# Pairing neighbouring attention-logit steps in two pairs of PSUM banks

## The chip, the cores and the metric

The kernel runs on one core of one Trainium2 chip. A core has five engines with a queue each: TensorE (PE, matmuls, with its weight loads shown as PEld), VectorE (DVE), ScalarE (ACT), GpSimd (POOL) and SyncE (SP), which issues the DMA transfers. The engines run on their own and meet through semaphores. Matmul results land in PSUM, which the kernel uses as eight banks of 128 x 512 fp32. The metric is the time of one execution on the device, in microseconds (us), as the median of the runs.

## What is computed

Two encoder layers run over a sequence of 512 tokens of width 1024. Layer 0 mixes tokens by differential attention, layer 1 by gated linear attention; in both, a four-head cross-attention into 256 memory tokens runs beside the mixer, then one output projection and a gated MLP follow. The change is in layer 0. Its mixer, cut to what matters:

```python
def diff_attention(q, k, v, ...):          # 6 heads, each with two maps m of width 64
    q = rms_norm(q, g0) * d ** -0.5; k = rms_norm(k, g1)
    for each block of 128 queries:
        logits = einsum('bhmqd,bhmkd->bhmqk', qb, k) + bias
        logits = where(key_chunk <= query_chunk, logits, -inf)
        p = softmax(logits)
        w = p[:, :, 0] - lam * p[:, :, 1]
        o = einsum('bhqk,bhkv->bhqv', w, v)
    return rms_norm(o, g) * (1 - lam_init)
```

The memory cross-attention has heads of width 64 as well, with logits of 128 queries by 256 memory tokens.

## The kernel before

All large products (the projections, the output projection, the MLP) split their fp32 operands into a high and a low part and issue three matmuls of 128x128 weights by 512 columns for each. These are called gemm matmuls here (lines L330 to L332 in `gemm`, L351 to L353 in `product`). The weights come from DRAM in blocks of 128x1024 or less; ScalarE makes the high part (L253) and VectorE the low part (L256).

In layer 0 the attention is woven into the gemm matmuls of the projections by a script, `SCRIPT`, read by `do` from left to right. A number fills in that many microseconds' worth of gemm matmuls from a queue `F` (by its own costing). A letter with a number issues one step. TensorE executes in exactly this order. The other engines' queues are ordered by the framework's scheduler when the program is built. The steps:

- `P` (`prepare`): four transposes of a head's q and four of its k on TensorE (helper at L220), each into one `ps_tp` bank; ScalarE copies each bank out (L682).
- `L` (`logits`, step t of 15): 64-row matmuls (L719), since a map has width 64. The two maps go to the upper and lower 64 rows and to two banks, tag `lg`. The steps group (head, query block) pairs so that one step fills up to 512 columns (`TOGETHER`); each step is 8, 12 or 16 matmul instructions on the chip. VectorE then adds the bias and finds the maximum, bank by bank (L726), ScalarE takes the exponential (L729), VectorE combines the two maps (L734, L735, L738).
- `T` (`turn`): four transposes of the combined weights into a `ps_tp` bank, copied out by ScalarE (L748).
- `V` (`values`): eight matmuls with v (L760) into an `sm` bank. The last `V` of a head starts `output`: four squares on ScalarE (L771).
- `s` (scale): VectorE normalises the head's output (L777, L779).
- `F` (`finish`): four transposes of a finished head into a `ps_tp` bank. ScalarE (L310) and then VectorE (L311) read it to make the high and low part for the output projection.
- `q`, `k`, `l`, `t`, `v`: the same for the memory cross-attention: normalisation (q0: L386, L387, L390) and transposed queries (q1, two groups of four transposes into `ps_tp`, copied at L582), keys into an `sm` bank, logits (L591, 64-row matmuls, eight per block, maximum at L599, exponential at L603), transposes into `ps_tp` (L616), values (L629).
- `N`, `a`, `b`, `X`, `O`, `!`: normalisation of q and k, operands of the memory projection, reloading x, the output projection (its sums are added at L1061), flushing the queue.

PSUM has four tags, `mm`, `sm`, `lg` and `tp`, with two banks each. A bank is free for the next user of its tag once its readers are done. `M`, `logits` with the tag `tp`, is defined among the steps and not used by the script.

In layer 1 the memory logits are issued two blocks at a time, one block in the `lg` banks and one in the `sm` banks.

Of the kernel before, what the change touches and what calls it, by code (L numbers as in the profile page):

```python
# [37 lines left out]

SCRIPT = """
    17.75 P0 3.9  # L40
    L0 a3 P1 8.45 a0 0.97
    L1 1.94 a1 T0
    L2 3.57 a2
    L3 T1 4.86 N2 V0 T2 N3 V1 12.33
    L4 P2 6.17 V2 T3
    L5 s0 T4 2.27 V3
    L6 P3 b1 V4 5.2 T5
    L7 T6 F0 7.14 b0
    L8 V5 T7 8.42 V6 s1 N5 N4 F1
    L9 V7 P4 b2 4.45 T8 T9 s2 3.0  # L50
    L10 V8 3.55 X P5 q0
    L11 b3 V9 T10 4.2
    L12 F2 V10 s3 T11 3.8 q1 k0
    L13 3.15 l0 V11 T12 3.65
    L14 F3 t0 3.3 V12 T13 t1 l1 3.9 T14 l2 t2 2.3 O k1 t3 s4 l3 v0 t4 V13 V14 t6 t5 1.3 t7 F4 v1 s5 F5 6.15 ! 4.55
"""

ORDER = (('v', 0), ('qk', 1), ('kv', 0), ('qk', 2), ('vm', 2), ('kv', 1))
# [28 lines left out]
def _pieces():  # L87

    plan = []

    def piece(key, name, i, ks, *ranges):
        plan.append((key, name, i, ks, ranges))

    for l in range(2):
        if l == 0:
            w = "w_in_diff"
            piece(("qk", 0), w, 0, K8, (0, 256), (768, 1024))
            for key in ORDER:
                if key[0] == "qk":
                    p = key[1]  # L100
                    piece(key, w, 0, K8, (256 * p, 256 * p + 256), (768 + 256 * p, 1024 + 256 * p))
                elif key[0] == "kv":
                    piece(key, "w_mem_kv", key[1], K8, (0, 512))
                elif key[0] == "vm":
                    p = key[1]
                    piece(key, w, 0, K8, (1536 + 256 * p, 1792 + 256 * p), (2304, 2560))
                else:
                    p = key[1]
                    piece(key, w, 0, K8, (1536 + 256 * p, 2048 + 256 * p))
        else:  # L110
            w = "w_in_gla"
            piece(("gm", 1), w, 0, K8, (2304, 2576))
            for c in range(5):
                piece(("g", c), w, 0, K8, (512 * c, min(512 * c + 512, 2304)))
        for i, part in enumerate(PASS[l]):
            for c, ks in part:
                piece(("o", l, i, c), "w_out", l, ks, (256 * c, 256 * c + 256))
        base = 0
        for nq in HALVES:
            for q in range(base, base + nq):  # L120
                piece(("ua", l, q), "w_up", l, K8, (256 * q, 256 * q + 256))
                piece(("ug", l, q), "w_up", l, K8, (DFF + 256 * q, DFF + 256 * q + 256))
            for c in range(4):
                piece(("dn", l, base, c), "w_down", l, tuple(range(2 * base, 2 * base + 2 * nq)),
                      (256 * c, 256 * c + 256))
            base += nq
    return plan


def _blocks():  # L130

    out = []
    for key, name, i, ks, ranges in _pieces():
        w = sum(b - a for a, b in ranges)
        step = WTILE // w
        out.append([(name, i, ks[j:j + step], ranges, w) for j in range(0, len(ks), step)])
    return out
# [42 lines left out]
def trunk(ctx, tc, head_d, x_t, mem_t, wpack, cols_a_d, cols_d, conv_d, gate_d, rel_bias, diff_lambda, consts, onehot, out):  # L180
# [12 lines left out]
    def bank(tag):  # L193
        return ps.tile([128, 512], F32, name=f"ps_{tag}", tag=tag)

    def xtile():
        return xs.tile([128, S], F32, name="xt", tag="xs", bufs=XS)
# [9 lines left out]
    def blk(b, w=128):  # L207
        return slice(w * b, w * b + w)
# [40 lines left out]
    plan, blocks, made = _pieces(), _blocks(), []  # L249
# [318 lines left out]
    class MemAttn:  # L568
# [13 lines left out]
                A.activation(self.qT[hp], p, AF.Copy, scale=c_mq(self.l))  # L582


        def logits(self, *blocks):
            banks = [(bank(tag), bank(tag)) for _, tag in zip(blocks, ("lg", "sm") if self.l else ("lg", "tp"))]
            for b, pl in zip(blocks, banks):
                for hp in range(2):
                    for j in range(2):
                        hh = blk(j, 64)  # L590
                        mm(pl[j][:, blk(hp, 256)], self.qT[hp][hh, blk(b)], kmT[self.l][hh, hp], start=True, stop=True)  # L591
            for b, pl in zip(blocks, banks):
                self.softmax(b, pl)
# [51 lines left out]
    def diff_layer(pool, mix, acc):  # L645
# [45 lines left out]
        def members(t):  # L691
            pr, s = divmod(t, len(TOGETHER))
            out, at = [], 0
            for j, i in TOGETHER[s]:
                out.append((2 * pr + j, i, 4 * j + i, at))
                at += 128 * (i + 1)
            return pr, out, at

        def bias(h):
            bt = heads[h]["bt"] = pool.tile([128, S], F32, name="bt", bufs=2)  # L700
            src = bass.AP(tensor=bias_d.tensor, offset=bias_d[h].offset + 1, ap=[[1, 128], [1, 512]])
            nc.sync.dma_start(bt, src)
            G.memset(bt[0:64, 0:64], -1e30)

        def logits(t, tag="lg"):
            pr, group, _ = members(t)
            P = pairs[pr]
            s2, nm, rc = P["s2"], P["nm"], P["rc"]
            for h, _, _, _ in group:
                if "bt" not in heads[h]:  # L710
                    bias(h)
            pls = bank(tag), bank(tag)
            for h, i, _, at in group:
                nk = 128 * (i + 1)
                cuts = (0, nk) if i == 0 else (0, nk // 2, nk)
                for k0, k1 in zip(cuts, cuts[1:]):
                    for m in range(2):
                        hh = blk(m, 64)
                        mm(pls[m][:, at + k0:at + k1], heads[h]["q"][hh, blk(i)], heads[h]["k"][hh, k0:k1],  # L719
                           start=True, stop=True)  # L720
            e = xtile(), xtile()
            for m in range(2):
                for h, i, g, at in group:
                    c = slice(at, at + 128 * (i + 1))
                    n1 = nm[:, 8 * m + g:8 * m + g + 1]
                    V.tensor_tensor_reduce(  # L726
                        out=e[m][:, c], in0=pls[m][:, c], in1=heads[h]["bt"][:, 127 + 128 * i::-1], scale=-1.0,
                        scalar=1e38, op0=ALU.add, op1=ALU.min, accum_out=n1)
                    A.activation(e[m][:, c], e[m][:, c], AF.Exp, scale=-1.0, bias=n1,  # L729
                                              accum_out=s2[:, m, g:g + 1])  # L730
            ids = sorted(g for _, _, g, _ in group)
            step = max(ids[-1] - ids[0], 1)
            b, lr = slice(ids[0], ids[-1] + 1, step), slice(8 + ids[0], 9 + ids[-1], step)
            V.reciprocal(rc[:, b], s2[:, 1, b])  # L734
            V.scalar_tensor_tensor(rc[:, lr], rc[:, b], nlam, s2[:, 0, b], op0=ALU.mult, op1=ALU.mult)  # L735
            for _, i, g, at in group:
                c = slice(at, at + 128 * (i + 1))
                V.scalar_tensor_tensor(e[1][:, c], e[1][:, c], rc[:, 8 + g:9 + g], e[0][:, c],  # L738
                                                    op0=ALU.mult, op1=ALU.add)
            live[t] = e[1]  # L740
# [57 lines left out]
        ma = MemAttn(pool, 0, qm, mix, False)  # L798
        ops, keys = [None] * 2, [None] * 2
        for key in ORDER:  # L800
# [16 lines left out]

        doing = {
            "L": logits, "M": lambda i: logits(i, "tp"), "T": turn, "V": values, "P": prepare, "F": finish,
            "N": lambda i: norms(i // 2, i % 2), "a": lambda i: ops[0]((2 * i, 2 * i + 1)),  # L820
            "b": lambda i: ops[1]((2 * i, 2 * i + 1)), "k": lambda i: keys[i]("sm"),
            "q": lambda i: ma.queries() if i else (F.need("v2"), ma.norm()),
            "l": lambda i: ma.logits(i), "t": ma.turn, "v": lambda i: ma.values(i, "sm"),
            "s": lambda i: scales.pop(i)(), "X": lambda i: load_x(x_t),
            "O": lambda i: last.append(out_proj(0, mix, 1, acc, 5)), "!": lambda i: F.flush()}
        do(SCRIPT, doing)
# [228 lines left out]
    def load_x(src):  # L1055
        for k in range(KT):
            xT[k] = xtile()
            nc.sync.dma_start(xT[k], src[k])
# [117 lines left out]
    for l in range(2):  # L1176
        with tc.tile_pool(name=f"at{l}", bufs=2) as pool:
            mix = [None] * 8
            sums, acc = acc, [None]
            if l == 0:  # L1180
                diff_layer(pool, mix, acc)
            else:
                gla_layer(pool, mix, sums)
                out_proj(1, mix, len(PASS[1]) - 1, acc)
                F.flush()
        with tc.tile_pool(name=f"ff{l}", bufs=2) as pool:
            acc = ffn(pool, l, acc)
# [73 lines left out]
```

## Time and profile before

| | |
|---|---|
| median of 3 runs | 1168.48 us (1168.42 to 1168.51) |
| the profiled execution | 1168.01 us |
| its span, first to last instruction | 1166.2 us |
| mean granted TensorE clock | 1.000 |
| logit matmuls of layer 0 (L719) | 168, first at 53.3, last at 188.3 us |

The profile of one execution gives the span in several views: busy time of each engine, the chain of work that ended last, groups of instructions by line, operation and tile ("out<-in", then the shapes, the count, the busy time and the mean duration in ns, and the idle time before them), and the order in time (start, duration, engine, line, operation, tiles, shapes, count; neighbouring equal instructions are merged). Matmuls overlap: the end of one is modelled, so the spacing of starts tells how long TensorE spends on each.

### The profile page before, as it was taken

How to read it: one execution, taken by the hardware profiler on the slowest of the kernel's cores; microseconds unless marked ns; L12 is line 12 of the kernel's file. 1: busy time of each engine (PE TensorE's matmuls, PEld its weight loads, DVE VectorE, ACT ScalarE, POOL GpSimd, SP SyncE). 2: the span in 40 equal slices, each digit the busy share in tenths (PEclk: the TensorE clock that was granted, in tenths of full speed). 3: DMA queues.
4: the chain of work that ended last, by engine and by line, in shares of the span. 5: the costliest groups of instructions: out<-in, count | busy, mean ns of one | idle time of the engine just before them, and what ended most of it. 6: DMA issues, size and time to landing. Idle time of an engine off the chain costs nothing.

```text
span 1166.2 us, 14790 instructions
## 1 busy us (share of the span) xinstructions
PE 1160.7 (100%) x5658; PEld 965.3 (83%) x5658; DVE 750.9 (64%) x1256; ACT 545.5 (47%) x951; POOL 5.0 (0%) x27
## 2 busy tenths in 40 slices
PE   9999999999999999999999999999999999999998
PEld 7888888888888888888888888988888888888887
DVE  7576778688677326677447637777876743576741
ACT  6676687555344213344437634436643421343420
POOL 0000000000000000000000000000000000000000
PEclk9999999999999999999999999999999999999999
DMA  8423242123223223222342230333232323232231
GB/s 295 158 70 99 78 141 73 63 103 130 85 90 120 83 88 124 75 91 98 120 148 68 81 108 3 110 121 109 93 123 73 98 102 108 85 114 73 89 101 45
DMA packets 39556, 117.68 MB, mean 101 GB/s; under 512 B 4703, under 2 KB 7192, under 8 KB 39486
## 3 DMA queue, kind: packets, MB, share of 16 engines
q1 hardware_dynamic: 39054, 116.35, 29.5%
q8 instruction: 44, 0.72, 0.3%
q10 hardware_dynamic: 432, 0.39, 0.1%
q14 instruction: 26, 0.21, 0.1%
HBM read 112.52 MB, written 4.21 MB: 100 GB/s over the span
## 4 chain that ended last, share of the span: by engine, by line
PE 98%; ACT 1%; DVE 1%; issue 0%; POOL 0%; DVEq 0%; POOLq 0%
PE ps_mm L352 9%; PE ps_mm L351 9%; PE ps_mm L353 9%; PE ps_sm L353 8%; PE ps_sm L352 8%; PE ps_sm L351 7%; PE ps_mm L330 6%; PE ps_mm L332 6%; PE ps_mm L331 6%; PE ps_tp L353 3%; PE ps_lg L353 3%; PE ps_lg L352 3%; PE ps_tp L352 3%; PE ps_lg L351 3%; PE ps_tp L351 3%; PE ps_tp L220 3%
## 5 line engine op out<-in xcount | busy, mean ns | idle before, releaser
L253 ACT CAST whi<-raw 128x1024 fp32r<-128x1024 f32 (+4 forms) x212 | 207.6, 986 | 245.4 <-PE ps_tp L352 120.9
L256 DVE TENSOR_TENSOR wlo<-raw,whi 128x1024 fp32r<-128x1024 f32 (+4 forms) x212 | 240.3, 1140 | 117.5 <-ACT whi L253 116.6
L351 PE MATMUL ps_mm<-xsh,whi 128*128 128x512 f32 x438 | 171.6, 392 | 0.0
L352 PE MATMUL ps_mm<-xsl,whi 128*128 128x512 f32 x438 | 170.6, 389 | 0.0
L353 PE MATMUL ps_mm<-xsh,wlo 128*128 128x512 f32 x438 | 170.5, 389 | 0.0
L351 PE MATMUL ps_sm<-xsh,whi 128*128 128x512 f32 x378 | 147.0, 389 | 0.0
L352 PE MATMUL ps_sm<-xsl,whi 128*128 128x512 f32 x378 | 147.0, 389 | 0.0
L353 PE MATMUL ps_sm<-xsh,wlo 128*128 128x512 f32 x378 | 147.0, 389 | 0.0
L330 PE MATMUL ps_mm<-whi,xsh 128*128 128x512 f32 (+2 forms) x336 | 129.1, 384 | 0.0
L332 PE MATMUL ps_mm<-whi,xsl 128*128 128x512 f32 (+2 forms) x336 | 126.1, 375 | 0.0
L331 PE MATMUL ps_mm<-wlo,xsh 128*128 128x512 f32 (+2 forms) x336 | 125.9, 375 | 0.0
L1113 ACT ACTIVATE cvo<-u,cv 128x512 f32<-128x512 f32 x88 | 71.4, 815 | 112.1 <-DVE u L1111 112.1
L352 PEld LDWEIGHTS ps_mm<-xsl,whi 128*128 128x128 f32 x438 | 82.3, 188 | 17.2 <-DVE xsl L311 0.4
L351 PEld LDWEIGHTS ps_mm<-xsh,whi 128*128 128x128 f32 x438 | 82.2, 188 | 17.1 <-issue 0.3
L353 PEld LDWEIGHTS ps_mm<-xsh,wlo 128*128 128x128 f32 x438 | 82.2, 188 | 17.1
L1114 DVE SCALAR_TENSOR_TENSOR cvo<-u,cv,cvo 128x512 f32<-128x512 f32 x88 | 65.7, 749 | 36.2 <-ACT cvo L1113 36.0
L352 PEld LDWEIGHTS ps_sm<-xsl,whi 128*128 128x128 f32 x378 | 70.9, 188 | 14.8
L351 PEld LDWEIGHTS ps_sm<-xsh,whi 128*128 128x128 f32 x378 | 70.9, 188 | 14.7
L353 PEld LDWEIGHTS ps_sm<-xsh,wlo 128*128 128x128 f32 x378 | 70.9, 188 | 14.7
L332 PEld LDWEIGHTS ps_mm<-whi,xsl 128*128 128x128 f32 x336 | 63.2, 188 | 11.6
L330 PEld LDWEIGHTS ps_mm<-whi,xsh 128*128 128x128 f32 x336 | 63.2, 188 | 11.3 <-ACT ks L659 0.3
L331 PEld LDWEIGHTS ps_mm<-wlo,xsh 128*128 128x128 f32 x336 | 63.3, 188 | 10.4
(295 smaller groups left out, 1760.1 us busy)
## 6 DMA issues: line engine op xcount, KB each, us to landing
raw<-in_wpack_dram SPq DMA_DIRECT2D x178, 512.0 KB, 3.5
xt<-in_x_t_dram SPq DMA_DIRECT2D x15, 256.0 KB, 5.2
raw<-in_wpack_dram SPq DMA_DIRECT2D x15, 256.0 KB, 3.0
raw<-in_wpack_dram SPq DMA_DIRECT2D x8, 384.0 KB, 3.0
xres<-xt SPq DMA_DIRECT2D x8, 256.0 KB, 3.0
xt<-xres SPq DMA_DIRECT2D x8, 256.0 KB, 5.4
out_dram<-xt SPq DMA_DIRECT2D x7, 256.0 KB, 2.0
bt<-bias_d SPq DMA_DIRECT2D x6, 256.0 KB, 4.1
```

The lines of the kernel that those rows point to most:

```text
L220: nc.tensor.transpose(dst, src, ident[:n, :n])
L253: ins = A.copy(hi[:, c], raw[:, c])
L256: V.tensor_sub(lo[:, c], raw[:, c], hi[:, c].bitcast(F32))
L330: mm(p, sh[k][:, blk(b)], hi, start=k == 0, stop=False)
L331: mm(p, sh[k][:, blk(b)], lo, start=False, stop=False)
L332: mm(p, sl[k][:, blk(b)], hi, start=False, stop=k == KT - 1)
L351: mm(p, hi[:, blk(n)], bh, start=i == first, stop=False)
L352: mm(p, hi[:, blk(n)], bl, start=False, stop=False)
L353: mm(p, lo[:, blk(n)], bh, start=False, stop=i == last)
L1113: A.activation(c, u[:, 2:], AF.Identity, scale=cv[l][:, 2, j:j + 1], bias=cv[l][:, 3, j:j + 1])
L1114: V.scalar_tensor_tensor(c, u[:, 1:S + 1], cv[l][:, 1, j:j + 1], c, op0=ALU.mult, op1=ALU.add)
```

## The change

Pairs of neighbouring logit steps stand directly behind each other. The first of a pair takes the two `lg` banks, the second the two `tp` banks (`M`, and `m` for the memory attention). The memory logits of blocks 1 and 2 are issued by one call. So the 64-row matmuls of layer 0 form eleven runs (L0 M1, L2 M3, L4, L5 M6, L7 M8, L9, L10 M11, L12 M13, L14 m0, l1 with block 2, l3) where there were nineteen (L0 to L14, l0 to l3). The matmuls and all other work stay the same in kind and number. The order of other steps in the script changes with it: P3 stands behind T3, F2 and T11 behind the fill of 3.8, F3 behind the fill of 3.3, P5 and q0 behind V9, and fills are cut up differently.

```diff
 SCRIPT = """
     17.75 P0 3.9
-    L0 a3 P1 8.45 a0 0.97
-    L1 1.94 a1 T0
-    L2 3.57 a2
-    L3 T1 4.86 N2 V0 T2 N3 V1 12.33
-    L4 P2 6.17 V2 T3
-    L5 s0 T4 2.27 V3
-    L6 P3 b1 V4 5.2 T5
-    L7 T6 F0 7.14 b0
-    L8 V5 T7 8.42 V6 s1 N5 N4 F1
+    L0 M1 a3 3.4 P1 5.05 a0 0.97
+    1.94 a1 T0
+    L2 M3 a2 3.57
+    T1 4.86 N2 V0 T2 N3 V1 12.33
+    L4 P2 6.17 V2 T3 P3 2.27 T4
+    L5 M6 s0 V3 b1 2.6 V4 2.6 T5
+    L7 M8 3.5 T6 F0 3.64 b0
+    V5 T7 8.42 V6 s1 N5 N4 F1
     L9 V7 P4 b2 4.45 T8 T9 s2 3.0
-    L10 V8 3.55 X P5 q0
-    L11 b3 V9 T10 4.2
-    L12 F2 V10 s3 T11 3.8 q1 k0
-    L13 3.15 l0 V11 T12 3.65
-    L14 F3 t0 3.3 V12 T13 t1 l1 3.9 T14 l2 t2 2.3 O k1 t3 s4 l3 v0 ...
+    L10 M11 V8 3.55 X b3 V9 P5 q0 T10 4.2
+    L12 M13 V10 s3 3.8 F2 T11 q1 k0
+    3.15 V11 T12 3.65
+    L14 m0 3.3 F3 V12 T13 t0 t1 l1 3.9 T14 t2 2.3 O k1 t3 s4 l3 v0 ...
 """
...
-        def logits(self, *blocks):
-            banks = [(bank(tag), bank(tag)) for _, tag in zip(blocks, ("lg", "sm") if self.l else ("lg", "tp"))]
+        def logits(self, *blocks, tags=None):
+            banks = [(bank(tag), bank(tag)) for _, tag in zip(blocks, tags or (("lg", "sm") if self.l else ("lg", "tp")))]
...
-            "l": lambda i: ma.logits(i), "t": ma.turn, "v": lambda i: ma.values(i, "sm"),
+            "l": lambda i: ma.logits(*((1, 2) if i == 1 else (i,))), "m": lambda i: ma.logits(i, tags=("tp",)),
+            "t": ma.turn, "v": lambda i: ma.values(i, "sm"),
```

More of the change, by code (lines that the diff above doesn't have):

```diff
@@ L40 @@
     17.75 P0 3.9
-    L0 a3 P1 8.45 a0 0.97
-    L1 1.94 a1 T0
-    L2 3.57 a2
-    L3 T1 4.86 N2 V0 T2 N3 V1 12.33
-    L4 P2 6.17 V2 T3
-    L5 s0 T4 2.27 V3
-    L6 P3 b1 V4 5.2 T5
-    L7 T6 F0 7.14 b0
-    L8 V5 T7 8.42 V6 s1 N5 N4 F1
-    L9 V7 P4 b2 4.45 T8 T9 s2 3.0
-    L10 V8 3.55 X P5 q0
-    L11 b3 V9 T10 4.2
-    L12 F2 V10 s3 T11 3.8 q1 k0
-    L13 3.15 l0 V11 T12 3.65
-    L14 F3 t0 3.3 V12 T13 t1 l1 3.9 T14 l2 t2 2.3 O k1 t3 s4 l3 v0 t4 V13 V14 t6 t5 1.3 t7 F4 v1 s5 F5 6.15 ! 4.55
+    L0 M1 a3 3.4 P1 5.05 a0 0.97
[6 more added lines that the diff above has]
+    V5 T7 8.42 V6 s1 N5 N4 F1
+    L9 V7 P4 b2 4.45 T8 T9 s2 3.0
+    L10 M11 V8 3.55 X b3 V9 P5 q0 T10 4.2
+    L12 M13 V10 s3 3.8 F2 T11 q1 k0
+    3.15 V11 T12 3.65
+    L14 m0 3.3 F3 V12 T13 t0 t1 l1 3.9 T14 t2 2.3 O k1 t3 s4 l3 v0 t4 V13 V14 t6 t5 1.3 t7 F4 v1 s5 F5 6.15 ! 4.55
 """
```

## The prediction

> **What bounds the kernel now.** I read the page first (shares, granted clock, chain), then the waits of TensorE, then the order in time around the logits.
>
> ```profile
> span 1166.2 us, 14790 instructions
> PE 1160.7 (100%) x5658; PEld 965.3 (83%) x5658; DVE 750.9 (64%) x1256; ACT 545.5 (47%) x951; POOL 5.0 (0%) x27
> PEclk9999999999999999999999999999999999999999
> PE 98%; ACT 1%; DVE 1%; issue 0%; POOL 0%; DVEq 0%; POOLq 0%
> ```
>
> ```profile
> PE ps_tp L446 <- POOL idle L443: 1.3, 1, 1.3
> ```
>
> TensorE is busy in 1160.7 of 1166.2 us, the chain that ends last is 98% TensorE, and its longest wait for another engine is the 1.3 us at the start. So time can be won only by making TensorE's own stream shorter, and every new wait of TensorE is lost one for one: no idle time downstream swallows it. That makes the question a balance of two sums: the mode changes that go, and the waits that come.
>
> **What the pairing removes.** The trace shows a single run of 64-row matmuls between gemm matmuls, and, in the second layer's memory attention, two steps of the same size already issued one behind the other.
>
> ```profile
> 64.61 0.39 PE L332 MATMUL ps_mm<-whi,xsl 128*128 128x512 f32 x1
> 64.93 1.14 PE L719 MATMUL ps_lg<-kT,qT 64*128 64x256 f32 x8
> 65.99 0.50 PE L330 MATMUL ps_mm<-whi,xsh 128*128 128x512 f32 x1
> 66.33 0.40 PE L331 MATMUL ps_mm<-wlo,xsh 128*128 128x512 f32 x1
> ```
>
> ```profile
> 637.46 0.39 PE L331 MATMUL ps_mm<-wlo,xsh 128*128 128x512 f32 x1
> 637.69 0.39 PE L332 MATMUL ps_mm<-whi,xsl 128*128 128x512 f32 x1
> 638.01 1.14 PE L591 MATMUL ps_lg<-kmT,xt 64*128 64x256 f32 x8
> 638.98 1.03 PE L591 MATMUL ps_sm<-kmT,xt 64*128 64x256 f32 x8
> 639.93 0.50 PE L330 MATMUL ps_mm<-whi,xsh 128*128 128x512 f32 x1
> 640.28 0.40 PE L331 MATMUL ps_mm<-wlo,xsh 128*128 128x512 f32 x1
> ```
>
> The first column is the start. A gemm matmul starts 0.23 us after the one before it (637.46 to 637.69). From the last gemm start to the second gemm start behind it is 66.33 - 64.61 = 1.72 us with eight 64-row matmuls between, and 640.28 - 637.69 = 2.59 us with sixteen. The second eight cost 0.87 us in a pair. In a run of their own they cost 1.72 less the two gemm pitches that would be there anyway, 1.72 - 0.46 = 1.26 us. A pair saves 0.39 us. Between transposes the same comparison reads
>
> ```profile
> 200.62 1.14 PE L591 MATMUL ps_lg<-kmT,xt 64*128 64x256 f32 x8
> 201.68 0.66 PE L220 MATMUL ps_tp<-C,xt 128*128 128x128 f32 x4
> ```
>
> ```profile
> 648.27 1.03 PE L220 MATMUL ps_tp<-C,xt 128*128 128x128 f32 x8
> 649.24 1.13 PE L591 MATMUL ps_lg<-kmT,xt 64*128 64x256 f32 x8
> 650.21 1.03 PE L591 MATMUL ps_sm<-kmT,xt 64*128 64x256 f32 x8
> 651.17 0.66 PE L220 MATMUL ps_tp<-C,xt 128*128 128x128 f32 x4
> ```
>
> two runs of 1.06 against one of 1.93: 0.19 inside, and the late entry (64.93 - 64.61 = 0.32 for 0.23) and exit (0.34 for 0.23, less behind transposes) of the run that is gone make about 0.34. Eight runs go (nineteen to eleven), so 8 x 0.34 to 8 x 0.39 = 2.7 to 3.1 us; I take 2.9, as removed runs stand beside both kinds. The matmuls themselves stay, all of them.
>
> [...]
>
> **What it adds: waits for the ps_tp banks.** Every transpose (P, T, F, q, t) writes one of two ps_tp banks. A paired step holds both until VectorE has read them (L726). The trace has no such wait, so each is counted from the order of the changed program's queues and the durations here. Four transposes take 0.44 us: eight from 648.27 to 649.24, less the late entry of 0.09. Four places, all where the script was also reordered, are not covered.
>
> *P3 behind T3.* P3 needs two banks, one of them T3's. ScalarE copies T3 only after the four squares that V2 releases, in the changed queue as in this one:
>
> ```profile
> 105.75 1.05 PE L760 MATMUL ps_sm<-vv,xt 128*128 128x128 f32 x8
> 106.63 0.60 PE L220 MATMUL ps_tp<-C,xt 128*128 128x128 f32 x4
> ```
>
> ```profile
> 106.39 0.37 ACT L771 ACTIVATE xt<-ps_sm,rs 128x128 f32<-128x128 f32 x1 [4.45 <-PE ps_sm L760]
> 107.77 0.60 ACT L748 COPY xt<-ps_tp 128x512 f32<-128x512 f32 x1
> ```
>
> V2 takes 0.88 us. T3 starts at 106.63; T3 and P3's first four transposes take 0.44 us each, so P3's second four are due at 107.51, and the bank is free at 107.77 + 0.60 = 108.37: a wait of 0.9 us. Before, the run of L5's logits stood there.
>
> *q1 behind F2 and T11.* The old script put F2 ahead of V10 and 3.8 us of gemm ahead of q1. The new one issues F2, T11 and q1's two groups with nothing between, and F2 stands behind the pair L12 M13. F2's bank is free after VectorE's L311, and VectorE's queue from L12's end to that L311 holds both softmaxes, qm's normalisation, three weight splits and one head's output:
>
> ```profile
> 169.93 0.42 DVE L726 CUSTOM_DVE_ANT_0 xt<-ps_lg,bt 128x256 f32<-128x256 f32 x1
> 170.27 0.42 DVE L726 CUSTOM_DVE_ANT_0 xt<-ps_lg,bt 128x256 f32<-128x256 f32 x1
> ```
>
> ```profile
> L726 DVE CUSTOM_DVE_ANT_0 xt<-ps_lg,bt 128x384 f32<-128x384 f32 x12 | 6.6, 553 | 0.1
> L726 DVE CUSTOM_DVE_ANT_0 xt<-ps_lg,bt 128x128 f32<-128x128 f32 x12 | 3.4, 285 | 0.0
> L390 DVE TENSOR_TENSOR qm<-qm,rs_y 128x1024 f32<-128x1024 f32 x2 | 2.4, 1224 | 0.0
> L738 DVE SCALAR_TENSOR_TENSOR xt<-xt,rcd 128x256 f32<-128x256 f32 x6 | 2.6, 482 | 0.1
> L256 DVE TENSOR_TENSOR wlo<-raw,whi 128x768 fp32r<-128x768 f32 x8 | 7.5, 953 | 1.0 <-ACT whi L253 1.0
> L256 DVE TENSOR_TENSOR wlo<-raw,whi 128x1024 fp32r<-128x1024 f32 x178 | 216.6, 1222 | 111.8 <-ACT whi L253 111.0
> L779 DVE TENSOR_TENSOR o<-ps_sm,rs 128x512 f32<-128x512 f32 x6 | 4.1, 689 | 0.1
> L311 DVE SCALAR_TENSOR_TENSOR xsl<-ps_tp,cols,xsh 128x512 fp32r<-128x512 f32 x12 | 8.9, 749 | 6.0 <-ACT xsh L310 6.0
> L228 DVE SCALAR_TENSOR_TENSOR rs_t<-rs_t,rs_v 128x4 f32<-128x4 f32 x22 | 3.6, 162 | 0.6
> ```
>
> Successive instructions overlap by 0.07 us (0.42 long, 0.34 apart), which I take off each mean. Four L726 of 256: 1.4. Two of 384 with two of 128: 1.4. L390: 1.15. L738 over 1024 columns in four pieces: 1.65. L256: 2 x 0.88 + 1.15 = 2.9. L779: 0.6. Thirteen small ones at 0.09: 1.2. L311: 0.75. Together 11.1 us. TensorE, counted from the same point (L12's end): M13 0.95, V10 0.9, eighteen gemm matmuls 4.1, F2, T11 and q1's first group 0.44 each: the second group is due after 7.3 us. It waits 3.8 us, part of it already in the first group (T11's copy). By the same rows the other pairs are covered: behind L7 M8, the tightest, VectorE's eight reads take 2.8 us from L7's end, and TensorE has M8 and twelve gemm matmuls, 3.7 us, before T6.
>
> *t0 behind F3 and T13.* The same with the pair L14 m0: two L726 of 512 columns, six more 512-wide passes (L599, L1061, L738, L607), all taken as 0.62 by the L779 row,, a 256-wide split, small ones and L311 make about 7.3 us from L14's end; TensorE has m0 0.95, fifteen gemm matmuls 3.5, F3, V12 and T13 1.8, together 6.3. Wait: 1.0 us.
>
> *T10 behind P5.* The L11 run that stood between is now with L10. T10's bank is that of qT, whose copy stands on ScalarE behind two weight casts:
>
> ```profile
> L253 ACT CAST whi<-raw 128x768 fp32r<-128x768 f32 x8 | 6.5, 832 | 5.1 <-PE ps_mm L352 4.9 <-PE ps_mm L332 0.2
> L682 ACT ACTIVATE qT<-ps_tp,cols 128x512 f32<-128x512 f32 x6 | 4.1, 678 | 0.0
> ```
>
> Bounds are 0 (casts done when P5 ends) and 1.5 us (one cast and qT fully ahead); 0.5 is my value, the casts being about half done. Small waits elsewhere (M8 for T5's copy, out-projection banks whose L1061 stands behind softmaxes): 0 to 0.6, taken as 0.3. SP and POOL keep their instructions in the same order, so no transfer is moved past another; VectorE and ScalarE queues are otherwise only permuted, with slack at 64% and 47%.
>
> **The sum.** -2.9 + 0.9 + 3.8 + 1.0 + 0.5 + 0.3 = +3.6 us. The profiled execution took 1168.01 us (span 1166.2 and 1.8 around it): 1171.6. The three timed runs lie 0.47 above it, at 1168.48: 1172.1.
>
> **Rivals.** *The clock drops in the new gap.* Around q1 TensorE would do little for some 4 us, and this trace shows what an idle end does:
>
> ```profile
> 1162.90:1165.40 2.50, 0.00 (x0) 0.00 (x0) 0.74 (x2) 0.00 (x0) 0.00 (x0) 1.00 0.30 105
> 1165.40:1166.20 0.80, 0.00 (x0) 0.00 (x0) 0.00 (x0) 0.00 (x0) 0.00 (x0) 0.55 0.00 0
> ```
>
> TensorE is idle from 1162.9, and the granted clock falls 2.5 us later (1.00, then 0.55). At half speed for 2.5 to 5 us, 1.3 to 2.5 us more is lost: 1173.4 to 1174.6. Against it: transposes interrupt the gap. [...]
>
> *F2's read is in time.* If VectorE reaches L311 of F2 within 7.3 us (splits done before the pair, when the weight casts run early), the 3.8 goes, and 2.8 of waits stand against 2.9 saved: 1168.4, no change. For it: VectorE is idle 36% of the span; against: the 11.1 us are instructions in a fixed queue, not waits. It decides from 3.6 us of shortening on.
>
> *All covers hold:* no new wait at all, 1168.5 - 2.9 = 1165.6. Against it speaks every one of the four countings.
>
> [...]
>
> **How the numbers follow.** Forecast as summed, 1170.8 to 1173.4, chance 0.61; clock drop or longer queues 0.15; no pairing gain 0.05; F2 in time or the waits half as long 0.12; covers hold 0.07. A measurement of this kernel tells 0.2% (2.3 us) from no change. So faster 0.07, within 0.2% 0.13 (the F2 rival and the short edge of the forecast), slower 0.80. The likeliest is 1172.1. The range takes in the clock rival and half-sized waits: 1169.4 to 1175.2.
>
> **What would show it.** Right: the waits of TensorE list L220 on ps_tp waiting for ACT L748 (about 107) and for DVE L311 (near 177 to 180, and near 197), 6 us or more together; L719 and L591 of the first layer appear in pairs, the eight-run saving near 2.9. Wrong: no such waits, PE busy to the same share and a span near 1163; or waits on other lines (weights, ps_mm), which would mean that I priced the wrong queue.

## The result, and the profile after

| | before | changed |
|---|---|---|
| median of 6 runs | 1168.49 us (1168.31 to 1169.61) | 1175.12 us (1173.07 to 1177.20) |
| ratio to before, 95% interval | | 1.0055 (1.0042 to 1.0068) |
| the profiled execution | 1168.01 us | 1175.54 us |
| its span | 1166.2 us | 1173.8 us |
| mean granted TensorE clock of the six changed runs | | 1.000 once, 0.997 to 0.999 five times |

The change makes the kernel slower by 6.6 us. The forecast was 1172.1, with 1169.4 to 1175.2 as its range: the sign is right, and the median lies just inside the upper edge, 3.0 us above the forecast. From the page of the changed kernel, the span, the busy times and the chain that ended last:

```profile
span 1173.8 us, 14781 instructions
PE 1162.4 (99%) x5658; PEld 967.8 (82%) x5658; DVE 749.6 (64%) x1256; ACT 545.1 (46%) x951; POOL 5.0 (0%) x27
PE 95%; DVE 2%; ACT 2%; issue 0%; DMA 0%; DVEq 0%
```

The same 5658 matmuls run, and TensorE's share of the chain fell from 98% to 95%: VectorE and ScalarE now stand in it with 2% each, where they had 1%. The waits of TensorE (line that waits, what for and for whose line; total, times, longest) name the places; its five longest rows are shown. Line numbers are up to two smaller than before: L218 is the transposes' old L220, L309 was L311, L746 was L748, L680 was L682, L1060 was L1061.

```profile
PE ps_tp L218 <- DVE xsl L309: 2.9, 2, 1.9
PE ps_tp L218 <- ACT xt L746: 2.1, 2, 1.3
PE ps_tp L444 <- POOL idle L441: 1.3, 1, 1.3
PE ps_mm L349 <- DVE xt L1060: 0.5, 1, 0.5
PE ps_tp L218 <- ACT qT L680: 0.3, 1, 0.3
```

Of these, only the third row was there before. The others are the four places of the prediction and one that it had among its small ones. In order of time on TensorE (start, duration, and in brackets the wait before and who ended it), P3 behind T3, T10 behind P5, and t0 behind F3 and T13:

```profile
107.25 0.60 PE L218 MATMUL ps_tp<-C,qs 128*128 128x128 f32 x4
108.60 0.66 PE L218 MATMUL ps_tp<-C,ks 128*128 128x128 f32 x4 [0.75 <-ACT xt L746]
...
164.01 0.60 PE L218 MATMUL ps_tp<-C,ks 128*128 128x128 f32 x4
164.96 0.66 PE L218 MATMUL ps_tp<-C,xt 128*128 128x128 f32 x4 [0.34 <-ACT qT L680]
...
199.41 0.60 PE L218 MATMUL ps_tp<-C,xt 128*128 128x128 f32 x4
200.94 1.09 PE L218 MATMUL ps_tp<-C,xt 128*128 128x128 f32 x8 [0.93 <-DVE xsl L309]
```

Four transposes take 0.44 us from start to start where nothing waits (F2's, 176.71 to T11's 177.15). So the three places lose 108.60 - 107.25 - 0.44 = 0.91, 164.96 - 164.01 - 0.44 = 0.51 and 200.94 - 199.41 - 0.44 = 1.09 us. The bracket is smaller than the loss, since the modelled end of a group lies behind its last start; the losses here are always taken from the starts. The fourth place, q1 behind F2 and T11:

```profile
177.15 0.60 PE L218 MATMUL ps_tp<-C,xt 128*128 128x128 f32 x4
179.07 0.66 PE L218 MATMUL ps_tp<-C,qm 128*128 128x128 f32 x4 [1.33 <-ACT xt L746]
181.66 1.12 PE L218 MATMUL ps_tp<-C,qm 128*128 128x128 f32 x4 [1.93 <-DVE xsl L309]
182.56 1.06 PE L218 MATMUL ps_sm<-C,xt 128*128 128x128 f32 x4
183.28 0.78 PE L328 MATMUL ps_mm<-whi,xsh 128*128 128x512 f32 x1
```

T11 starts at 177.15, q1's first group 1.48 us later than T11's transposes allow, its second group 179.07 to 181.66, 2.15 us later: 3.6 us in all. The first of them is predicted as well: that bank is T11's, whose copy stands behind two weight casts and F2's L308 on ScalarE. VectorE's queue over the same time begins and ends with

```profile
170.83 0.42 DVE L724 CUSTOM_DVE_ANT_0 xt<-ps_lg,bt 128x256 f32<-128x256 f32 x1 [1.22 <-PE ps_lg L717]
...
173.24 1.22 DVE L388 TENSOR_TENSOR qm<-qm,rs_y 128x1024 f32<-128x1024 f32 x1
...
180.86 0.74 DVE L309 SCALAR_TENSOR_TENSOR xsl<-ps_tp,cols,xsh 128x512 fp32r<-128x512 f32 x1
```

and none of its rows between the first and the last shows a wait: 180.86 + 0.74 - 170.83 = 10.8 us of plain work, for which 11.1 were counted. The last two rows of the TensorE fence above show something else: four transposes of 1.06 us instead of 0.60, and a gemm matmul behind them of 0.78 where it otherwise takes 0.48 to 0.49 there. The windows of that place (length; busy time and count of TensorE, weight loads, VectorE, ScalarE, GpSimd; granted clock; share and rate of the DMA):

```profile
177.00:181.18 4.18, 1.40 (x11) 0.93 (x9) 4.18 (x13) 2.71 (x4) 0.00 (x0) 1.00 0.47 151
181.18:184.59 3.41, 2.93 (x11) 2.74 (x12) 0.42 (x1) 1.37 (x2) 0.00 (x0) 0.50 0.16 50
```

In 4.18 us TensorE was busy for 1.40, and then the granted clock was 0.50 for 3.41 us. The clock rival came on top of the forecast. TensorE was not idle throughout: in the 3.41 us in front of the drop (177.77 to 181.18), which begin as T11's transposes end, it was busy for 0.66.

The rest of the profiled execution's 7.5 us is at its start, in front of everything that the change touches. Before, then changed:

```profile
5.26 0.63 PE L516 MATMUL ps_sm<-whi,xsh 128*128 128x512 f32 x2
```

```profile
5.56 1.05 PE L514 MATMUL ps_sm<-whi,xsh 128*128 128x512 f32 x2
```

The same two matmuls take 0.63 and 1.05 us, and from their start to the next one's 0.47 (5.26 to 5.73) and 0.85 (5.56 to 6.41): the first ones run at about half pace, in the changed kernel's execution until about 7.1 us, while in the other this is over by 5.26. That costs 0.8 us here (the same matmul, the first single one into `ps_sm`, starts at 9.10 and 9.93). The granted clock is 1.00 from 4.00 to 7.50 us in both. The end of this half pace differs from execution to execution: in the profiled one of nowait below, two such matmuls still take 0.63 us at 6.31, and 0.46 from 6.94 on.

### The profile page after: what moved, and what is told of

The parts are those of the page before. It is cut to its first block, busy times and chain, and to the rows that moved or that the text cites. A ratio compares the mean times of both kernels' runs of the same rounds, so it can differ in the third digit from the quotient of the medians.

```text
span 1173.8 us, 14781 instructions
## 1 busy us (share of the span) xinstructions
PE 1162.4 (99%) x5658; PEld 967.8 (82%) x5658; DVE 749.6 (64%) x1256; ACT 545.1 (46%) x951; POOL 5.0 (0%) x27
## 4 chain that ended last, share of the span: by engine, by line
PE 95%; DVE 2%; ACT 2%; issue 0%; DMA 0%; DVEq 0%
PE ps_mm L350 8%; PE ps_mm L349 8%; PE ps_mm L351 8%; PE ps_sm L350 7%; PE ps_sm L351 7%; PE ps_sm L349 7%; PE ps_mm L328 6%; PE ps_mm L330 6%; PE ps_mm L329 6%; PE ps_lg L350 3%; PE ps_tp L350 3%; PE ps_tp L351 3%; PE ps_lg L351 3%; PE ps_tp L349 3%; PE ps_lg L349 3%; PE ps_tp L218 2%
## 5 line engine op out<-in xcount | busy, mean ns | idle before, releaser
L328 PE MATMUL ps_mm<-whi,xsh 128*128 128x512 f32 (+2 forms) x336 | 129.7, 386 | 0.0
L328 PEld LDWEIGHTS ps_mm<-whi,xsh 128*128 128x128 f32 x336 | 63.5, 189 | 11.4 <-issue 0.7
```

Source lines behind the costliest of these rows:

```text
L328: mm(p, sh[k][:, blk(b)], hi, start=k == 0, stop=False)
```

## The experiments

Each time is the median of 5 to 11 executions, taken beside the kernel before in two sessions; the kernel before took 1168.38 us (median of 21) in the first and 1168.21 (of 19) in the second. Changed lines of the script are shown against the changed kernel, unless it says otherwise. The first four runs ask what each wait costs; A stands there for the theory that the waits are what the prediction counted.

**f2gap: q1 gets its cover back.**

```diff
-    L12 M13 V10 s3 3.8 F2 T11 q1 k0
-    3.15 V11 T12 3.65
+    L12 M13 V10 s3 2.5 F2 T11 4.45 q1 k0
+    V11 T12 3.65
```

> Theory A (the four ps_tp waits, the clock drop in the one at q1, against 2.9 us saved): 4.45 us of gemm now stand between T11 and q1, so F2's bank is free in time. The 3.7 us of wait near 177 to 182 and the drop to half clock go together: 1175.1 - 3.7 - 1.7 = 1169.7 us (1168.8 to 1170.5), granted clock 1.000 after the start, runs within 1 us of each other. Rival B (pairing loads VectorE and ScalarE, and a wait removed turns up at the next transposes): 1172 us or more, with new waits behind q1.

Measured: 1169.99 us (1169.67 to 1173.67), ratio 1.0016 (1.0007 to 1.0025). In order of time on TensorE, T11, the first and last of the 21 gemm matmuls, and q1:

```profile
175.52 0.60 PE L218 MATMUL ps_tp<-C,xt 128*128 128x128 f32 x4
175.88 0.48 PE L328 MATMUL ps_mm<-whi,xsh 128*128 128x512 f32 x1
...
180.51 0.39 PE L351 MATMUL ps_mm<-xsh,wlo 128*128 128x512 f32 x1
180.74 1.03 PE L218 MATMUL ps_tp<-C,qm 128*128 128x128 f32 x8
```

Both waits of q1 are gone, and ten of eleven runs have a mean clock of 0.999 or 1.000. The one place costs 1175.12 - 1169.99 = 5.1 us: 3.6 of waits, and about 1.5 of clock.

**f2half: a third of the cover.**

```diff
-    L12 M13 V10 s3 3.8 F2 T11 q1 k0
-    3.15 V11 T12 3.65
+    L12 M13 V10 s3 3.8 F2 T11 1.3 q1 k0
+    1.85 V11 T12 3.65
```

> 1.3 us of gemm between T11 and q1 instead of none. Theory A: 1.3 us of the wait go. If the clock is lost only after some 2.5 to 3.4 us with hardly any work, the remaining wait of about 2.5 us in two parts no longer costs the clock: 1175.1 - 1.3 - 1.7 = 1172.1 (1171.3 to 1173), clock 1.000. If the clock drop is not bound to the length of the gap (rival), it stays: 1173.8 and a clock row of 0.5 near 181.

Measured: 1173.44 us (1171.65 to 1174.19), ratio 1.0038 (1.0025 to 1.0051); the mean clock is 1.000 in four of five runs. So the clock is kept, with a third of the cover, and the time lies between the two that were expected. The 2.5 us of the expectation stand in the trace before (idle from 1162.90 to 1165.40), the 3.4 in the changed one (177.75 to 181.18). At the place itself theory A holds: from T11's start to the seventh gemm matmul behind it pass 5.36 us (177.00 to 182.36) instead of 8.21 (177.15 to 185.36), so 2.85 us are gone where 3.0 were expected. The profiled run, the slowest of the five, carries a wait that neither theory had: 1.1 us at 622 us, in layer 1 (below). Whether the other four carry it is not shown. The question of the clock went on to a cleaner test, busygap.

**p3late: P3 moved back behind gemm matmuls.**

```diff
-    L4 P2 6.17 V2 T3 P3 2.27 T4
+    L4 P2 3.9 V2 T3 2.27 P3 2.27 T4
```

> 2.27 us of gemm between T3 and P3. Theory A: the wait of 0.9 us at 107 for T3's copy goes and nothing else changes: 1174.2 us. Rival B: the wait moves to T4 or L5 and the time stays at 1175.1.

Measured: 1174.73 us (1174.13 to 1175.86), ratio 1.0053 (1.0041 to 1.0066). In its waits of TensorE the L746 row falls from 2.1 us in two waits to 1.3 in one: the wait at P3 is gone. The median moved by 0.4 us, within the scatter of either kernel, which the clock at q1 makes larger than the effect. The window of the half clock in its profiled run is twice as long as the changed kernel's:

```profile
179.00:185.83 6.83, 5.70 (x18) 4.83 (x19) 1.50 (x3) 2.51 (x6) 0.00 (x0) 0.50 0.16 58
```

It begins during q1's second wait, as there, but 1.1 us ahead of its end, not 0.5. At half pace its 5.70 busy us cost up to 2.9 us, where the 2.93 of the changed kernel cost up to 1.5. In this execution the longer drop takes back what the wait at P3 gave, so the price of that wait rests on its row and not on the time.

**nowait: the same eleven runs, another script around them.** The pairs stay, and fills, F, T, q and P are moved so that no bank is late by the countings of the prediction. The whole script is rearranged; its core, with the lines regrouped:

```diff
-    L4 P2 6.17 V2 T3 P3 2.27 T4
-    L10 M11 V8 3.55 X b3 V9 P5 q0 T10 4.2
-    L12 M13 V10 s3 3.8 F2 T11 q1 k0
-    3.15 V11 T12 3.65
-    L14 m0 3.3 F3 V12 T13 t0 t1 l1 3.9
+    L4 P2 4.87 V2 T3 2.6 P3 3.57 T4
+    s2 3.0 P5 1.3 L10 M11 0.65 V8 1.6 X b3 V9 q0 T10 4.2
+    L12 M13 V10 s3 2.5 T11 F2 3.9 q1
+    2.9 V11 k0 T12
+    L14 m0 2.65 T13 1.3 t0 F3 0.65 V12 t1 1.3 l1 3.9
```

> The same eleven runs, with the steps between the pairs put where, by the rows' durations, no bank is waited for. Theory A: only the saving is left, 1168.5 - 2.8 = 1165.7 us (1165.2 to 1166.3), faster than both; TensorE waits for nothing in layer 0. Rival B: 1168 or more, waits on ps_tp remain because a pair holds both banks.

Measured: 1166.71 us (1165.74 to 1167.91), ratio 0.9984 (0.9975 to 0.9993). Faster than both kernels, by 1.7 us against the kernel before: the pairing does save time, once hardly anything waits for it (d128, below, tests whether it is the pairing or the new order). It saves less than the 2.9 us of the prediction. Its waits of TensorE are the one at the start and three in layer 1, of which the longest is shown:

```profile
PE ps_tp L444 <- POOL idle L441: 1.3, 1, 1.3
PE ps_lg L908 <- DVE xsh L898: 0.5, 1, 0.5
```

**d64 and d128: the price of a change of mode by itself.** On the script of nowait, a dummy matmul of 128 columns stands ahead of the second step of every pair, in a bank that the step then overwrites. In d64 it is two 64-row matmuls, in d128 one of 128 rows, which parts the run (64*128 and 128*128 in the rows).

```diff
+    def dummy(pl):                     # d64
+        for m in range(2):
+            hh = blk(m, 64)
+            mm(pl[m][:, :128], ident[hh], ident[hh], start=True, stop=True)
```

```diff
+    def dummy(pl):                     # d128
+        mm(pl[0][:, :128], ident, ident, start=True, stop=True)
```

> The version without waits, with two 64-row dummy matmuls of 128 columns (one per half of the rows) ahead of the second step of each of the eight pairs, in the bank that the step then overwrites. No computed value changes. Eight 64-row matmuls of 256 columns take 0.95 us behind others of their kind, so the two dummies take about 0.12 us; eight places make 1.0 us: 1166.7 + 1.0 = 1167.7 by either theory, as the tiling mode stays. This is the yardstick for the run with 128-row dummies.

> The same with one 128-row dummy matmul of 128 columns in each of the eight places: the same columns through the array (eight such take 1.05 us, 0.13 each), but each pair is parted by a matmul of the other mode. Theory (a run of 64-row matmuls of its own costs 0.25 to 0.39 us): 2.0 to 3.1 us above the run with 64-row dummies, 1169.7 to 1170.8. Rival (a run costs nothing of itself, and the kernel without waits is faster for another reason, its script): equal to the 64-row run, 1167.7.

Measured: d64 1169.22 us (1168.35 to 1171.18), d128 1171.40 us (1170.52 to 1172.17); ratios 1.0008 (0.9999 to 1.0017) and 1.0026 (1.0016 to 1.0036). L0 and M1 in order of time, d64 first:

```profile
54.59 1.14 PE L726 MATMUL ps_lg<-kT,qT 64*128 64x192 f32 x12
55.57 0.39 PE L223 MATMUL ps_tp<-C 64*128 64x128 f32 x4
55.79 1.03 PE L726 MATMUL ps_tp<-kT,qT 64*128 64x256 f32 x8
56.75 0.50 PE L333 MATMUL ps_mm<-whi,xsh 128*128 128x512 f32 x1
```

```profile
54.69 1.14 PE L724 MATMUL ps_lg<-kT,qT 64*128 64x192 f32 x12
55.76 0.49 PE L221 MATMUL ps_tp<-C 128*128 128x128 f32 x2
56.18 1.14 PE L724 MATMUL ps_tp<-kT,qT 64*128 64x256 f32 x8
57.24 0.50 PE L331 MATMUL ps_mm<-whi,xsh 128*128 128x512 f32 x1
```

From the pair's start to the gemm matmul behind it pass 2.16 and 2.55 us, and 1.94 in nowait without a dummy. The dummies themselves take the same time: 0.22 us for the 64-row pair (55.57 to 55.79), and two 128-row instructions at the pace of the transposes, 0.11 each. So the difference, 0.39, is the cost of leaving the mode and coming back. Seven of the eight pairs show it (0.37 to 0.39); at L5 and M6 it is 0.24, as d64 waits 0.16 there. It has the size of the prediction's upper price, though that was read between gemm matmuls. The medians differ by 2.2 us, not by 8 x 0.39 = 3.1: with its dummies d64 has waits again, which the longer runs of d128 cover. Its profiled run has this one, and d128's has none on `ps_tp` in layer 0:

```profile
PE ps_tp L218 <- ACT xt L608: 0.8, 1, 0.8
```

Both lie above the numbers expected, by 0.6 and 1.5 us, since a dummy takes 0.22 us and not 0.12 or 0.13, and d64 by that wait besides. The rival, a price of nothing, is out. Nor is the new order the reason of nowait's gain, by an estimate from these rows: d128 has nowait's order with every pair parted, and without the 1.8 us of its eight dummies it would take 1169.6 us, more than the kernel before. The 0.39 make about 0.2 us for each of the two changes of mode. What the 0.2 consists of, no run here shows.

**busygap: work in the gap.** Three dummy matmuls of 512 columns into a bank that nobody reads.

```diff
-    L12 M13 V10 s3 3.8 F2 T11 q1 k0
+    L12 M13 V10 s3 3.8 F2 T11 D q1 k0
+        def busy(i):
+            p = bank("lg")
+            for _ in range(3):
+                mm(p, ident, C, start=True, stop=True)
```

> The changed kernel with three dummy matmuls of 512 columns (0.88 us each, 2.6 us) between T11 and q1, where TensorE waits 1.5 and 2.1 us. Their bank is read by nobody and no computed value changes. Theory (the idleness of the gap makes the clock drop to half for 3.4 us, which costs about 2 us): the dummies lie inside the waits, the clock stays at 1.000, and the time falls by 1.5 to 2 us in spite of the added work, 1173.1 to 1173.6. Rival (the drop has another cause, or costs nothing): 1175.1 or more, and the mean clock stays at 0.997 to 0.999.

Measured: 1173.67 us (1173.29 to 1174.36), ratio 1.0047 (1.0034 to 1.0059), 1.45 us below the changed kernel and 0.1 above what was expected, with a mean clock of 1.000 in four of five runs. The same stretch as above, in windows:

```profile
177.00:181.20 4.20, 3.76 (x17) 2.04 (x15) 4.20 (x13) 2.42 (x4) 0.00 (x0) 1.00 0.46 153
181.20:184.60 3.40, 2.94 (x17) 2.59 (x18) 0.40 (x1) 1.97 (x5) 0.00 (x0) 1.00 0.16 47
```

TensorE is busy 3.76 instead of 1.40 us, the clock stays at 1.00, and 17 matmuls are done in the second window instead of 11. q1's second group starts at 181.66 in both, so the waits are as long as before and only the clock differs. From there to the fourth gemm matmul pass 1.63 us (to 183.29) instead of 3.00 (to 184.66): the half clock costs 1.4 us in the profiled execution, and about 1.5 in the median. More work, less time: here it was the idleness that took the clock away.

**lessdve: VectorE's queue made shorter.** VectorE's multiplication of qm by its norm is left out in layer 0, so the memory attention sees queries that are not normalised.

```diff
-        V.tensor_mul(yv, yv, r.unsqueeze(2).to_broadcast([128, nb * ng, d]))
+        if scaled:                       # False for layer 0's qm
+            V.tensor_mul(yv, yv, r.unsqueeze(2).to_broadcast([128, nb * ng, d]))
```

> The changed kernel without VectorE's multiplication of the memory queries qm by their norm in layer 0 (1.22 us, in VectorE's queue between L12's end and F2's L309); the memory attention then sees queries that are not normalised. Theory (the second wait at q1 is the length of VectorE's queue): that wait falls from 1.9 to 0.8 us and the time by about 1.1 us, to 1174.0, or by up to 3 us where the shorter gap also keeps the clock up. Rival (the wait is for ScalarE's copies or for something else): no change, 1175.1, the wait still 1.9 us.

Measured: 1174.21 us (1172.60 to 1175.89), ratio 1.0052 (1.0040 to 1.0065). In order of time, q1's two groups:

```profile
178.80 0.66 PE L218 MATMUL ps_tp<-C,qm 128*128 128x128 f32 x4 [1.33 <-ACT xt L747]
180.56 0.79 PE L218 MATMUL ps_tp<-C,qm 128*128 128x128 f32 x4 [1.10 <-DVE xsl L309]
181.14 1.06 PE L218 MATMUL ps_sm<-C,xt 128*128 128x128 f32 x4
```

The first group's wait stays at 1.33 us, as ScalarE's queue is untouched. The second falls from 1.93 to 1.10 us, by 0.83, less than the 1.1 expected. VectorE's L309 starts 9.20 us behind L12's first read (170.56 to 179.76) instead of 10.03 (170.83 to 180.86), 0.83 sooner as well: the wait follows the length of VectorE's queue. The median falls by 0.9 us, though the scatter of both kernels is wider than that. The clock still drops (1.06 for four transposes): waits of 1.48 and 1.32 us, taken from the starts, are enough.

## Why the prediction came out so

**The four waits: right, in place, cause and size.** P3 0.91 for 0.9, T10 0.51 for 0.5, q1 3.6 for 3.8, t0 1.09 for 1.0; together 6.1 for 6.2 us. f2gap and p3late took two of them away by giving the cover back, lessdve shortened one by shortening the queue that it was counted from.

**The small waits: too small, 1.3 us for 0.3.** The ones taken as 0 to 0.6 lie here:

```profile
111.02 1.14 PE L717 MATMUL ps_lg<-kT,qT 64*128 64x192 f32 x12
111.99 1.19 PE L717 MATMUL ps_tp<-kT,qT 64*128 64x256 f32 x8
...
123.39 1.39 PE L717 MATMUL ps_tp<-kT,qT 64*128 64x192 f32 x12
...
207.19 0.39 PE L351 MATMUL ps_mm<-xsh,wlo 128*128 128x512 f32 x1
208.08 0.50 PE L349 MATMUL ps_mm<-xsh,whi 128*128 128x512 f32 x1 [0.50 <-DVE xt L1060]
```

An `M` behind a T has to wait for that step's copy out of the `tp` bank while its own run is under way: M6 is 1.19 us long instead of 1.03 (0.16), and M8 is later by 0.35 (from the starts of its matmuls); ScalarE's copy of T5 ends at 123.60, when M8 has begun. The gemm matmuls that wait for L1060 lose 208.08 - 207.19 - 0.23 = 0.66 at 207 and 0.16 at 197. The prediction named both kinds and took them together as 0.3.

**The saving: the term that was too large.** The prediction took 0.34 to 0.39 us for each run that goes, eight times. In the starts of the matmuls, summed from the first gemm matmul behind 20 us to the first values of the memory attention, with the waits named above and the half clock taken off:

```
                            before   changed   nowait
logit runs                   20.36     18.76    18.93
transposes                   18.40     17.98    17.51
values                       11.95     11.58    11.44
gemm, above 0.2275 each       3.13      3.41     3.98
sum against before                     -2.11    -1.98
gemm stretches                  24        26       33
```

(us; the changed kernel's sum is less 7.5 of waits and 1.4 of half clock; nowait's holds two small waits, 0.15 and 0.3.) The same sum gives 2.2 for f2gap and 2.1 for busygap, whose traces have no half clock. Inside the runs the eight pairs bring what was read off the trace, 1.6 us or 0.2 each. Of the other part, the late entry and exit, 1.3 us were counted and 0.5 came. No run isolates why, but the places suggest it: of the eight runs that go, only L1 stood between two gemm stretches. The other seven had transposes or values on one side or both, and these still stand there and have an entry of their own. In nowait, for one:

```profile
173.72 0.60 PE L218 MATMUL ps_tp<-C,o 128*128 128x128 f32 x4
174.08 0.48 PE L328 MATMUL ps_mm<-whi,xsh 128*128 128x512 f32 x1
174.39 0.39 PE L329 MATMUL ps_mm<-wlo,xsh 128*128 128x512 f32 x1
```

A gemm matmul behind transposes holds TensorE for 174.39 - 174.08 = 0.31 us where the next takes 0.23, much as one behind a logit run (0.34). Transposes and gemm matmuls are both 128*128, so a late start of this size needs no change of tiling mode, while the prediction counted it as a price of one. And the new script cuts the gemm matmuls into 26 stretches where there were 24. So a break does cost some 0.39, as d128 shows, but the change removes not eight such breaks: it removes eight runs out of places that mostly stay broken. The term is 2.1, not 2.9.

**The sum once more.** -2.1 + 6.1 + 1.3 = +5.3 for +3.6 predicted. To this the profiled execution adds 1.4 for its half clock and 0.8 for the start: +7.5, as measured (1175.54 - 1168.01). Without the start it is +6.7, and the medians differ by 6.6. So the forecast is 3.0 us short: about 0.8 by the saving, 1.0 by the small waits and 1.4 by the clock, all in the same direction. That the median still lies in the range is in part luck: the upper end was set for the clock rival, and not for two more terms that are off the same way, and the median ends 0.1 us inside it.

**The clock: the rival that came true besides.** It was given 0.15 and priced at 1.3 to 2.5 us, for 2.5 to 5 us at half speed, lengths that were the author's estimate. The profiled execution shows it, for 3.41 us. Four of the other five runs probably have it too: the five take 1174.52 to 1177.20 us at a mean clock of 0.997 to 0.999, and the sixth takes 1173.07 at 1.000. The mean alone does not prove it: it is 0.999 in nowait's profiled run too, whose gemm matmuls keep 0.23 us from start to start around q1 (178.28). busygap puts its price at 1.45 in the median. The case against it, that transposes interrupt the gap, was wrong: four of them, 0.66 us of work in 3.41, did not keep the clock up. *F2 in time* and *all covers hold* are out by the waits themselves; *no pairing gain*, given 0.05, by d128. What the second of these would have brought, 1165.6, nowait nearly has: 1166.7.

**What stays open.** f2half and the profiled run of f2gap have a wait of about 1.0 us in layer 1 (L328 for L848 on ScalarE, at 619 to 622 us), which the profiled executions of before, after and nowait do not have; lessdve has 0.6 and d128 0.3 of it. In f2gap VectorE's chain stands there behind one instruction:

```profile
616.90 0.55 DVE L891 TENSOR_TENSOR xsl<-xt,xsl 32x384 fp32r<-32x384 f32 x1 [1.92 <-ACT xsl L890]
```

Why ScalarE's L890 is late in some executions was not tried.

## What to carry to other kernels

Grouping steps of one tiling mode saved 0.2 us inside each pair here; of the entries and exits 0.5 us came where 1.3 were counted, by the author's reading because the neighbours of most runs that went kept a break of their own. Count the stretches of every kind before and after, not the runs alone. Banks that came free late were paid for by the steps that used them next, 6.1 us in four places, so follow the releasing engine's whole queue and put independent matmuls into that time: the same eleven runs cost 6.6 us in one script and gained 1.7 in another. And where waits left TensorE busy for 0.66 to 1.28 of 3.41 us here, the half clock came on top, 1.4 us in the changed kernel: add it to their price.

## What was not expected of the hardware

The granted clock fell to 0.50 although TensorE was not idle throughout, and with no single wait over 2.2 us (2.15, from the starts): in the 3.41 us in front of the three drops that were profiled it had been busy for 0.66 (changed kernel), 1.04 (lessdve) and 1.28 us (p3late). The clock stayed down for 3.41 us in the changed kernel, for 6.83 in p3late and for about 3.4 in lessdve (by the pace of its rows, 180.95 to 184.35), and each time it fell during q1's second wait or within 0.4 us of its end. With one long wait of 1.8 us (f2half), where the least busy 3.41 us (178.10 to 181.51) still have 1.53 of work, it stayed at 1.00, as it did with 3.76 of 4.20 us busy (busygap). And adding 2.6 us of useless matmuls made a kernel 1.45 us faster.
